# W_in's rows scaled by norm_mix, weights loaded ahead of x, a fixed TensorE order for the first row products, one PSUM layout through mix_out

## The chip, the cores and the metric

The kernel runs on one core of a Trainium2 chip. The metric is the device time of one execution in microseconds (us). An engine is named TensorE (PE), VectorE (DVE), ScalarE (ACT), GpSimd (POOL) or SyncE (SP, which issues most loads). Before the change three runs took 1360.5, 1361.68 and 1362.62 us; the median, 1361.68 us, is the time before.

## What is computed

One decoder layer on x (1024 tokens by 1024 channels, float32) with a memory of 256 tokens. Cut to what the change touches:

```python
def rms_norm(x, g):
    y = x * rsqrt(mean(x * x, axis=-1) + EPS)
    return y * g

hn = rms_norm(h, norm_mix)
proj = hn @ w_in                       # 1024 x 2320
gq, gk, gv, gr, ga, sq, sk, sv = split(proj)
o_gla = gla_mixer(gq, gk, gv, gr, ga, w_alpha, b_alpha, gla_gain)
o_swa = swa_mixer(sq, sk, sv, rel_bias, sinks)
h = h + concat([o_gla, o_swa]) @ w_out
h = h + cross_attn(rms_norm(h, norm_cross), rms_norm(mem, norm_mem), w_q_c, w_k_c, w_v_c, w_o_c)
h = h + conv_ffn(rms_norm(h, norm_ffn), w_up, conv_w, conv_b, w_down)
return rms_norm(h, norm_final)
```

`gla_mixer` is gated linear attention in chunks of 64 tokens, `swa_mixer` attention in a window of 128 tokens.

## The kernel before

**Number form.** A float32 product is made of three matmuls on a high and a low part of each operand (`mm3`: high by high, high by low, low by high). `split` makes the parts: ScalarE writes the rounded high part (L109, or L112 with a gain), DVE subtracts it from the source (L110, or L113 with a gain). A weight is loaded by SP into a stage tile `st` (L121) and split into two `w` tiles.

**Start (`rows_a`).** x arrives as eight tiles of 128 tokens (`load_x`; tiles `gr` and `prob`). TensorE transposes them into PSUM banks of the role S (`prepare_x`, L385), in groups of 1, 1, 2, 2 and 2 tiles. Each bank is copied to a tile `pts` (L388), which POOL writes to DRAM as `xt_d` (L389; it is read again for the residual), and which `split` turns, with norm_mix as gain, into the parts of x (L112, L113). `row_tile` then makes 24 matmuls per token tile, with x as the left operand and 272 columns of W_in on the right, for `ga`, `sv` and `gva`; each of these is scaled by the token's factor `rstd_x` when it leaves PSUM (L440, L442). The weights for it are nine DMAs, in three stage tiles (`row_weights`). SP issues x tile 0 first, then these nine, then x tiles 1 to 7.

**What sets the order.** In `rows_a` the tile framework's scheduler orders each engine; only the stretches under `manual_schedule` (the GLA) keep the order of the code. Each engine runs its own queue in order, so an instruction that waits holds all behind it. POOL's queue at the start holds the identity, the loads of the vectors (`vrows`, L234), the writes of `xt_d` and the masks for the attention (`masks`, L249 to L254); DVE's holds `mask_att` (L256), which reads a mask.

**After that.** `cols_swa` and `cols_gla` make the other projections transposed, a tile of 128 columns at a time, with 48 matmuls of 512 tokens; the windowed attention runs among them. The pool p2 follows, with its own PSUM layout: `gla_gates` (whose first transposes are L529), `gla_decays` (L573), `rows_b` (384 more columns of V, L136 to L138 with 384 columns), and `gla`. `gla` calls `memory`, a generator: its first part loads the two memory tiles, scales them by row (L313), transposes them (L320) and splits them into `wg`; the next parts make V (two banks of 512) and K (256 wide) of the memory for the cross attention, between the GLA's own steps, and store them through `la`. `mix_out` multiplies by W_out. `add_residual` (L866 to L874) gives the new residual, its parts `act` and its squares' sum `ss`. `rstd_of_sum` (L201, eight matmuls of one column each) and `rsqrt` (L170 and on) turn `ss` into the tokens' factors; `cross` starts with products on `act`.

**PSUM.** There are eight banks, shared by roles. Before, p1 has F=3, S=4, O=1; p2 has F=2, S=4, O=2; from mix_out on it is F=3, S=3, T=1, O=1. A pool's first use of a bank waits for the last use of the banks it lies over.

Of the kernel before, what the change touches and what calls it, by code (L numbers as in the profile page):

```python
# [16 lines left out]
F32 = mybir.dt.float32  # L18
F32R = mybir.dt.float32r
# [3 lines left out]
ALU = mybir.AluOpType  # L23
# [3 lines left out]
P = 128  # L27
# [13 lines left out]
GROUPS = (1, 1, 2, 2, 2)  # L41
# [19 lines left out]
class Layer:  # L61
# [67 lines left out]
    def load_cols(self, w, c0):  # L129

        src = w.rearrange("(kt p) c -> p kt c", p=P)[:, :, c0:c0 + P]
        return self.load([(lambda t: t, src)])
# [95 lines left out]
    def vectors(self, group, new):  # L228

        nc, base = self.nc, self.vec_at  # L230
        v = new("vrows", [P, P], bufs=2)
        at = 0
        for nm, src, n in group:
            nc.gpsimd.dma_start(out=v[at:at + n, :], in_=src.rearrange("o (n p) -> (o n) p", p=P))  # L234
            self.col[nm] = base + at
            at += n
        ps = self.bank("O")
        nc.tensor.transpose(ps[:, :at], v[:at, :], self.ident[:at, :at])
        nc.vector.tensor_copy(out=self.vec[:, base:base + at], in_=ps[:, :at])
        self.vec_at += at  # L240

    def masks(self, keep):
# [13 lines left out]
        nc.vector.tensor_scalar(out=self.mask_att, in0=self.mask_cum, scalar1=16.0, scalar2=None, op0=ALU.mult)  # L256

# [41 lines left out]
    def memory(self, new):  # L299
# [14 lines left out]
        parts = [[new("wg", [P, 3, MEM], F32R, 8) for _ in range(3)] for _ in range(2)]  # L314
        mh, ml = ([p[k // 3][:, k % 3] for k in range(NK)] for p in parts)
# [50 lines left out]
    def prepare_x(self, new):  # L366
# [4 lines left out]
        self.rstd_bc = self.bc_tile("rbx")  # L371
        self.xt_d = self.dram.tile([NK, P, T], F32, name="xt_d")
        self.x = [(self.xnew("x", dt=F32R, bufs=16), self.xnew("x", dt=F32R, bufs=16)) for _ in range(NK)]
        self.xact = self.whole(self.x)
        self.x_copies = []
        at = 0
        for n in GROUPS:
            sl = slice(at * P, (at + n) * P)
            m = 4 // n
            for k in range(0, NK, m):  # L380
                ps = self.bank("S")
                for q in range(m):
                    for i in range(n):
                        c = (q * n + i) * P
                        nc.tensor.transpose(ps[:, c:c + P], self.xr[at + i][:, (k + q) * P:(k + q + 1) * P], self.ident)  # L385
                xt = new("pts", [P, 512], bufs=9)
                copy = nc.scalar.copy if k // m % 2 else nc.vector.tensor_copy
                self.x_copies.append(copy(out=xt, in_=ps))  # L388
                nc.gpsimd.dma_start(out=self.xt_d[k:k + m, :, sl].rearrange("k p t -> p k t"),  # L389
                                    in_=xt.rearrange("p (k t) -> p k t", k=m))  # L390
                for q in range(m):
                    hi, lo = self.x[k + q]
                    h, l = self.split(xt[:, q * n * P:(q + 1) * n * P], hi[:, sl], lo[:, sl],
                                      self.v("norm_mix", k + q))
            with self.tc.issue_after(h.ins), self.tc.issue_after(l.ins):
                for i in range(at, at + n):
                    self.sumsq(self.xr[i], ssq[:, i:i + 1], T)
                self.rsqrt(self.rstd[:, at:at + n], ssq[:, at:at + n], D, n)
            yield range(at, at + n)
            at += n  # L400
            if at % 4 == 0:
                self.broadcast_rows(self.rstd, self.rstd_bc, [at // 4 - 1])


    def row_weights(self, cols, ks=range(NK), alloc=None):
# [5 lines left out]
        for g in range(ks.start, ks.stop, step):  # L411
# [5 lines left out]
            h, l = self.load(pieces, (P, m, n), alloc)  # L417
# [4 lines left out]
    def row_tile(self, i, weights, evac):  # L422

        n, hs, ls = weights
        ps = self.bank("F")
# [5 lines left out]
    def rows_a(self, keep, new):  # L431
# [13 lines left out]
        self.load_x(keep, new, range(1))  # L445
        groups = self.prepare_x(new)
        group = next(groups)
        with self.tc.issue_after(self.x_copies[0].ins), self.tc.issue_after(self.x_copies[1].ins):
            weights = self.row_weights([(1536, 16), (2192, 128), (512, 128)])
        self.load_x(keep, new, range(1, NT))  # L450
        while group:
            for i in group:
                self.row_tile(i, weights, evac)
            group = next(groups, None)

    def rows_b(self, new, first):
# [7 lines left out]
        n, hs, ls = self.row_weights([(640, 384)], range(4, NK), lambda s, sh: new("wg", sh, F32R, 8))  # L464
        for i in range(NT):
            self.row_tile(i, (n, first[1] + hs, first[2] + ls), evac)
# [29 lines left out]
    def cols_gla(self, keep):  # L496
# [3 lines left out]
        for tiles, tag, c0, n, scale in ((self.gr, "gr", 1024, 4, 1.0), (self.gk, "gk", 256, 2, 1.0),  # L500
                                         (self.gq, "gq", 0, 2, 0.125)):
            for t in range(n):
                dst = keep(tag, bufs=n)
                tiles.append(dst)
                yield from self.cols_parts(dst, self.load_cols(w, c0 + P * t), scale)

    def cols_swa(self, new):

        w = self.a["w_in"][0]
        self.sk = self.cols_in(new("sk"), self.load_cols(w, 2064), 1.0)  # L510
        self.sq = []
        wr = w.rearrange("(kt p) c -> p kt c", p=P)
        for t in range(4):
            pieces = [(lambda s, g=g: s[:, :, 64 * g:64 * g + 64],
                       wr[:, :, 1552 + 256 * g + 64 * t:1552 + 256 * g + 64 * t + 64]) for g in range(2)]
            self.sq.append(self.cols_in(new("sq", bufs=4), self.load(pieces), 0.125))
# [66 lines left out]
    def gla(self, new):  # L583
# [11 lines left out]
        memory = self.memory(new)  # L595
        next(memory)
        with self.tc.manual_schedule(engines={mybir.EngineType.PE}):
# [3 lines left out]
            for i, (early, late) in zip(range(0, NT, 2), ((2, 0), (2, 2), (2, 2), (2, 1))):  # L601
# [726 lines left out]
    def run(self):  # L1328
# [3 lines left out]
        with self.pool("xpool", "right") as self.xnew:  # L1332
            with self.pool("keep") as keep:
                with self.pool("p1") as new, self.banks(F=3, S=4, O=1):
                    self.constants()
                    self.vectors(self.vec_rows[:1], new)
                    self.rows_a(keep, new)
                    self.vectors(self.vec_rows[1:7], new)
                    self.vectors(self.vec_rows[7:], new)
                    self.masks(keep)  # L1340
                    self.swa_bias(new)
                    self.cols_swa(new)
                    self.gate_silu(self.swa(new, self.cols_gla(keep)))
# [16 lines left out]
        with psums:  # L1360
# [63 lines left out]
```

## Time and profile before

| | before |
|---|---|
| median of three runs | 1361.68 us |
| lowest, highest | 1360.5, 1362.62 us |
| the profiled execution's own time | 1360.55 us |
| its span in the profile | 1358.8 us |
| mean granted TensorE clock | 0.992 of full |
| TensorE busy | 1320.4 us (97%) |
| DVE, ScalarE, POOL busy | 899.9, 593.7, 84.7 us |
| chain that ended last | 90% TensorE, 3% DVE, 3% DMA, 2% ScalarE |

Times in the profile count from the start of the span, and the execution's own time holds 1.75 us more than the span. The chain that ended last is followed back from the last instruction, at each step to what released it. An idle time stands with the instruction that ended it, and with what that instruction had waited for. The granted clock is a share of TensorE's full speed.

### The profile page before, as it was taken

To read this page: it belongs to the slowest core of one execution; us is meant where nothing else is said; L and a number is where in the kernel's file an instruction comes from. 1 tells how busy PE (TensorE), PEld (TensorE's weight loads), DVE (VectorE), ACT (ScalarE), POOL (GpSimd) and SP (SyncE) were. 2 spreads that over 40 slices of the span, in tenths; PEclk is the share of its full clock that TensorE was granted. 3 is DMA by queue.
4 is the path that set the end of the run, shared out by engine and by line. 5 is a ranking of instruction groups with operands and counts; after the bars stand their busy time and mean duration, and the time that the engine had idled before them with its cause. 6 is when DMAs were issued, how large, how long until landed. Compare 5 with 4: busy or idle time off the path is not lost.

```text
span 1358.8 us, 17462 instructions
## 1 busy us (share of the span) xinstructions
PE 1320.4 (97%) x6635; PEld 1093.1 (80%) x6635; DVE 899.9 (66%) x1578; ACT 593.7 (44%) x1075; POOL 84.7 (6%) x142
## 2 busy tenths in 40 slices
PE   5999999999999999999999999999999999999997
PEld 5887777887888888888888888888888887888785
DVE  4626554546744444354449998888888887997776
ACT  5614546524533233354333644444444444454455
POOL 3100111000110000000110000000000000000000
PEclk8999999999999999999999999999999999999998
DMA  9442211114784511123330343222222228810203
GB/s 269 113 121 61 61 55 59 63 62 128 242 243 148 171 47 62 48 98 119 94 94 16 109 155 111 79 81 87 94 85 71 78 93 314 290 62 8 70 20 144
DMA packets 141389, 146.89 MB, mean 108 GB/s; under 512 B 15714, under 2 KB 108024, under 8 KB 141304
## 3 DMA queue, kind: packets, MB, share of 16 engines
q1 hardware_dynamic: 129974, 111.02, 26.6%
q0 software_dynamic: 10144, 32.63, 6.9%
q10 hardware_dynamic: 1186, 2.12, 0.4%
q8 instruction: 52, 0.85, 0.3%
q14 instruction: 33, 0.27, 0.1%
HBM read 109.03 MB, written 38.28 MB: 108 GB/s over the span
## 4 chain that ended last, share of the span: by engine, by line
PE 90%; DVE 3%; DMA 3%; ACT 2%; issue 1%; POOL 0%; SPq 0%; ACTq 0%; DVEq 0%; POOLq 0%
PE psS L1059 13%; PE psF L1059 13%; PE psF L136 12%; PE psF L138 12%; PE psF L137 12%; PE psF L1166 5%; PE psS L1166 5%; PE psT L1166 2%; PE psO L1166 2%; PE psO L136 1%; PE psS L136 1%; PE psS L138 1%; PE psS L137 1%; PE psO L137 1%; PE psO L138 1%; DMA act<-in_w_down_dram 1%
## 5 line engine op out<-in xcount | busy, mean ns | idle before, releaser
L109 ACT CAST w<-st 128x1024 fp32r<-128x1024 f32 (+2 forms) x165 | 145.1, 879 | 314.4 <-PE psF L137 158.5
L110 DVE TENSOR_TENSOR w<-st,w 128x1024 fp32r<-128x1024 f32 (+2 forms) x165 | 166.6, 1010 | 97.7 <-ACT w L109 95.9
L136 PE MATMUL psF<-x,w 128*128 128x512 f32 x336 | 132.6, 395 | 0.9 <-PE psS L705 0.9
L138 PE MATMUL psF<-x,w 128*128 128x512 f32 x336 | 131.3, 391 | 0.0
L137 PE MATMUL psF<-x,w 128*128 128x512 f32 x336 | 131.2, 390 | 0.0
L1088 DVE SCALAR_TENSOR_TENSOR uy<-uy,vec,uy 128x1023 f32<-128x1023 f32 (+1 forms) x88 | 112.0, 1279 | 1.3 <-ACT uy L1086 0.9
L1166 PE MATMUL psF<-w,w 128*128 128x512 f32 x330 | 92.6, 390 | 0.0
L1166 PE MATMUL psS<-w,w 128*128 128x512 f32 x330 | 92.2, 389 | 0.0
L1059 PE MATMUL psS<-a,w 128*128 128x512 f32 x360 | 86.6, 389 | 0.0
L1059 PEld LDWEIGHTS psS<-a,w 128*128 128x128 f32 x360 | 67.5, 188 | 14.3 <-ACT c L1067 0.3
L1059 PE MATMUL psF<-a,w 128*128 128x512 f32 x324 | 77.8, 389 | 0.0
L136 PEld LDWEIGHTS psF<-x,w 128*128 128x128 f32 x336 | 63.1, 188 | 16.7 <-issue 3.1
L138 PEld LDWEIGHTS psF<-x,w 128*128 128x128 f32 x336 | 63.1, 188 | 14.2 <-issue 0.6
L137 PEld LDWEIGHTS psF<-x,w 128*128 128x128 f32 x336 | 63.2, 188 | 12.6
L1166 PEld LDWEIGHTS psF<-w,w 128*128 128x128 f32 x330 | 61.8, 188 | 13.6 <-DVE w L110 0.6
L1166 PEld LDWEIGHTS psS<-w,w 128*128 128x128 f32 x330 | 61.9, 188 | 12.9
L1059 PEld LDWEIGHTS psF<-a,w 128*128 128x128 f32 x324 | 60.8, 188 | 12.6
L136 PE MATMUL psF<-act,w 128*128 128x512 f32 x176 | 69.5, 395 | 0.0
L137 PE MATMUL psF<-act,w 128*128 128x512 f32 x176 | 69.1, 392 | 0.0
L138 PE MATMUL psF<-act,w 128*128 128x512 f32 x176 | 68.7, 390 | 0.0
L1086 ACT ACTIVATE uy<-uy,vec 128x1024 f32<-128x1024 f32 x44 | 54.8, 1246 | 24.7 <-DVE uy L1079 16.9
L1059 PE MATMUL psS<-act,w 128*128 128x512 f32 x240 | 57.8, 389 | 0.0
(361 smaller groups left out, 2821.8 us busy)
## 6 DMA issues: line engine op xcount, KB each, us to landing
st<-in_w_up_dram SPq DMA_DIRECT2D x44, 512.0 KB, 4.7
g_d<-uy POOLq DMA_DIRECT2D x22, 512.0 KB, 2.9
act<-in_w_down_dram SPq DMA_DIRECT2D x12, 512.0 KB, 8.1
st<-g_d SPq DMA_DIRECT2D x10, 512.0 KB, 4.3
res<-g_d SPq DMA_DIRECT2D x10, 512.0 KB, 10.8
st<-in_w_in_dram SPq DMA_DIRECT2D x9, 512.0 KB, 4.3
xt_d<-pts POOLq DMA_DIRECT2D x16, 256.0 KB, 2.9
ow_d<-pts POOLq DMA_DIRECT2D x32, 128.0 KB, 2.7
```

The source lines that it names most:

```text
L109: h = nc.scalar.copy(out=hi, in_=src)
L110: l = nc.vector.tensor_tensor(out=lo, in0=src, in1=hi.bitcast(F32), op=ALU.subtract)
L136: mm(out, lhsT=lh, rhs=rh, start=start, stop=False)
L137: mm(out, lhsT=lh, rhs=rl, start=False, stop=False)
L138: mm(out, lhsT=ll, rhs=rh, start=False, stop=stop)
L1059: nc.tensor.matmul(ps, lhsT=b[l][:, q], rhs=a[q][r], start=first and q == 0 and n == 0, stop=first and q == 3 and n == 2, skip_group_check ...
L1086: nc.scalar.activation(out=y, in_=u, func=AF.Identity, scale=self.v("cw2", j), bias=self.v("conv_b", j))
L1088: nc.vector.scalar_tensor_tensor(out=y[:, s:], in0=u[:, :T - s], scalar=self.v(nm, j), in1=y[:, s:], op0=ALU.mult, op1=ALU.add)
L1166: nc.tensor.matmul(ps[i], lhsT=g[:, l, tk], rhs=w[:, r], start=first and k == 0 and m == 0, stop=first and k == n - 1 and m == 2, skip_gro ...
```

## The change

- norm_mix is no longer multiplied into x. Each stage tile of W_in is multiplied by the channel gains on DVE before it is split (`load` with `gains`, L124). The gain vector is loaded by ScalarE's queue instead of POOL's, and the masks are built on POOL ahead of everything else there.
- SP issues the nine weight loads before any x tile.
- A transposed bank of x is split straight from PSUM, 512 values wide (L109, L110 of the new file); no `pts` copy is made at the start. For `xt_d`, `save_x` adds high and low part (16 DVE additions, L404) and POOL writes the sums.
- TensorE's order there is written out: transposes of tiles 0 and 1, products of tile 0, transposes of tile 2, products of tile 1, and so on; the banks alternate between the roles F and O. Both halves of the factors are broadcast afterwards.
- One PSUM layout, F=2, S=4, O=2, holds from the start through mix_out. The layout F=3, S=3, T=1, O=1 opens only before `cross`.
- The memory's first part is called before `rows_b`. Its `wg` tiles are ordered by groups of channels. In the V products the two matmul triples of one bank follow each other before those of the other bank, where they alternated before. In the last round of the GLA's loop two parts of the memory, not one, run between `gla_output` and the products, so two parts are left for the end and not three.

```diff
-    def load(self, pieces, shape=(P, NK, P), alloc=None, parts=1):
+    def load(self, pieces, shape=(P, NK, P), alloc=None, parts=1, gains=None):
...
+        if gains is not None:
+            self.nc.vector.tensor_tensor(out=st, in0=st, in1=gains.unsqueeze(2).to_broadcast(list(shape)),
+                                         op=ALU.mult)
...
-        parts = [[new("wg", [P, 3, MEM], F32R, 8) for _ in range(3)] for _ in range(2)]
-        mh, ml = ([p[k // 3][:, k % 3] for k in range(NK)] for p in parts)
+        parts = [[new("wg", [P, 3, MEM], F32R, 8) for _ in range(2)] for _ in range(3)]
+        mh, ml = ([parts[k // 3][s][:, k % 3] for k in range(NK)] for s in range(2))
...
-                for q in range(2):
-                    for i in range(2):
-                        tk = slice(i * P, (i + 1) * P)
+                for i in range(2):
+                    tk = slice(i * P, (i + 1) * P)
+                    for q in range(2):
...
+        for i in range(NT):
+            tk = slice(i * P, (i + 1) * P)
+            for k in range(0, NK, 4):
+                ps = self.bank("S").rearrange("p (k t) -> p k t", k=4)
+                for q in range(4):
+                    nc.tensor.transpose(ps[:, q], self.xr[i][:, (k + q) * P:(k + q + 1) * P], self.ident)
+                h, l = self.split(ps, xh[:, k:k + 4, tk], xl[:, k:k + 4, tk])
...
+    def save_x(self, new):
...
+        for k, (hi, lo) in enumerate(self.x):
+            for h in range(2):
+                sl = slice(512 * h, 512 * h + 512)
+                t = new("pts", [P, 512], bufs=9)
+                self.nc.vector.tensor_tensor(out=t, in0=hi[:, sl].bitcast(F32), in1=lo[:, sl].bitcast(F32), op=ALU.add)
+                self.nc.gpsimd.dma_start(out=self.xt_d[k, :, sl], in_=t)
...
         self.xr = []
-        self.load_x(keep, new, range(1))
...
+        weights = self.row_weights([(1536, 16), (2192, 128), (512, 128)])
+        self.load_x(keep, new, range(NT))
+        tiles = self.prepare_x()
+        with self.tc.manual_schedule(engines={mybir.EngineType.PE}):
+            next(tiles)
+            for i in range(NT):
+                if i < NT - 1:
+                    next(tiles)
+                self.row_tile(i, weights, evac, "FO"[i % 2])
+        self.broadcast_rows(self.rstd, self.rstd_bc)
...
-            for i, (early, late) in zip(range(0, NT, 2), ((2, 0), (2, 2), (2, 2), (2, 1))):
+            for i, (early, late) in zip(range(0, NT, 2), ((2, 0), (2, 2), (2, 2), (2, 2))):
...
-                with self.pool("p1") as new, self.banks(F=3, S=4, O=1):
-                    self.constants()
-                    self.vectors(self.vec_rows[:1], new)
+                psums.enter_context(self.banks(F=2, S=4, O=2))
+                self.constants()
+                with self.pool("p1") as new:
+                    self.vectors(self.vec_rows[:1], new, self.nc.scalar)
+                    self.masks(keep)
                     self.rows_a(keep, new)
...
-                with self.pool("p2") as new, self.banks(F=2, S=4, O=2):
+                with self.pool("p2") as new:
                     self.gla_gates(new)
                     self.gla_decays(new)
-                    self.rows_b(new, first)
-                    self.gla(new)
+                    n, hs, ls = self.row_weights([(640, 384)], range(4, NK), lambda s, sh: new("wg", sh, F32R, 8))
+                    memory = self.memory(new)
+                    next(memory)
+                    self.rows_b(new, (n, first[1] + hs, first[2] + ls))
...
-            psums.enter_context(self.banks(F=3, S=3, T=1, O=1))
...
-        with psums:
+        psums.close()
+        with self.banks(F=3, S=3, T=1, O=1):
```

What moves on the engines shows in the order of their instructions, at three places. In these rows a line number is that of the file the rows are from (the new file's lines stand some four lines later), then the operation, what it writes and reads, and its size.

**DVE at the start.** Before, from the sixth split of x tile 1 (L113) on; `mask_att` waits for POOL's masks.

```order
L113 SCALAR_TENSOR_TENSOR x_106<-pts_232,vec,x_105 128x128
L113 SCALAR_TENSOR_TENSOR x_108<-pts_232,vec,x_107 128x128
L113 SCALAR_TENSOR_TENSOR x_116<-pts_138,vec,x_115 128x128
L388 COPY pts_304<-psS_299 128x512
L256 TENSOR_SCALAR mask_att_683<-mask_cum_681 128x128
L170 TENSOR_SCALAR rs_v_151<-ssq_97 128x1
L113 SCALAR_TENSOR_TENSOR x_110<-pts_248,vec,x_109 128x128
```

After, from the gain vector's copy on (`st` are the weights' stage tiles, `w` their low parts, `xl` the low part of x):

```order
L243 COPY vec<-psO_89 128x8
L260 TENSOR_SCALAR mask_att_94<-mask_cum_92 128x128
L124 TENSOR_TENSOR st_107<-st_107,vec 128x816
L124 TENSOR_TENSOR st_116<-st_116,vec 128x816
L124 TENSOR_TENSOR st_125<-st_125,vec 128x544
L110 TENSOR_TENSOR w_113<-st_107,w_112 128x816
L110 TENSOR_TENSOR xl_156<-psS_157,xh_155 128x4x128
L110 TENSOR_TENSOR w_122<-st_116,w_121 128x816
```

`mask_att` has moved ahead of the weights and of all splits of x; the gains stand ahead of the first split.

**DVE at the end of the row products.** After the change, between x tile 7's last split and the low half `w_610` of the first column tile's weight:

```order
L404 TENSOR_TENSOR pts_919<-xh_155,xl_156 128x512
L180 TENSOR_TENSOR rs_t_484<-rs_t_484,rs_v_483 128x2
L404 TENSOR_TENSOR pts_922<-xh_155,xl_156 128x512
L181 TENSOR_SCALAR rs_t_484<-rs_t_484 128x2
L404 TENSOR_TENSOR pts_925<-xh_155,xl_156 128x512
L182 TENSOR_TENSOR rstd_x<-rs_y_485,rs_t_484 128x2
L404 TENSOR_TENSOR pts_928<-xh_155,xl_156 128x512
L445 TENSOR_SCALAR sv_105<-psF_493,rstd_x 128x128
L445 TENSOR_SCALAR gva_106<-psF_493,rstd_x 128x128
L110 TENSOR_TENSOR w_610<-st_606,w_609 128x1024
```

The additions for `xt_d` are new here; six of the 16 stand before this weight, two of them ahead of these rows.

**TensorE at the cross start.** Before, from the last mix_out product on; `psO_4312` are the column sums, which run four at a time:

```order
L138 MATMUL psF_4278<-x_2656,w_4241 128x512
L201 MATMUL psO_4312<-ones,ss_3691 128x1 x4
L136 MATMUL psF_4359<-act_3692,w_4355 128x512
L137 MATMUL psF_4359<-act_3693,w_4355 128x512
L138 MATMUL psF_4359<-act_3692,w_4356 128x512
```

and 15 products further on:

```order
L138 MATMUL psF_4359<-act_4000,w_4355 128x512
L201 MATMUL psO_4312<-ones,ss_3691 128x1 x4
L136 MATMUL psF_4359<-act_4000,w_4355 128x512
L137 MATMUL psF_4359<-act_4001,w_4355 128x512
L138 MATMUL psF_4359<-act_4000,w_4356 128x512
```

After:

```order
L142 MATMUL psF_4225<-x_2673,w_4188 128x512
L205 MATMUL psO_4259<-ones,ss_3638 128x1 x8
L140 MATMUL psF_4310<-act_3639,w_4306 128x512
L141 MATMUL psF_4310<-act_3640,w_4306 128x512
L142 MATMUL psF_4310<-act_3639,w_4307 128x512
```

All eight sums now stand ahead of the first cross product.

## Rows read from the trace of the kernel before

**Rows 1.** The page, section 1: busy time, share of the span, instructions of each engine.

```profile
PE 1320.4 (97%) x6635; PEld 1093.1 (80%) x6635; DVE 899.9 (66%) x1578; ACT 593.7 (44%) x1075; POOL 84.7 (6%) x142
```

**Rows 2.** The chain of waits, 0 to 100 us: start, length, what.

```profile
2.26 4.34 DMA st<-in_w_in_dram
6.61 5.96 DMA gr<-in_x_dram
...
21.76 0.49 POOL xt_d L389
...
25.46 0.29 DVE mask_att L256
```

**Rows 3.** Timeline of TensorE, 4 to 54.6 us: start, length, instruction, [idle before <-releaser].

```profile
5.69 1.97 PE L385 MATMUL psS<-ident,gr 128*128 128x128 f32 x8
10.79 2.79 PE L385 MATMUL psS<-ident,gr 128*128 128x128 f32 x11 [3.13 <-DMA gr<-in_x_dram]
...
26.12 0.60 PE L138 MATMUL psF<-w,x 128*128 128x272 f32 x1 [6.48 <-DVE x L113]
...
45.48 1.91 PE L385 MATMUL psS<-ident,prob 128*128 128x128 f32 x16
...
52.81 0.29 PE L138 MATMUL psF<-w,x 128*128 128x272 f32 x1
...
54.07 0.40 PE L136 MATMUL psF<-x,w 128*128 128x512 f32 x1
```

**Rows 4.** Groups by shape on DVE, 5 to 54 us: busy us, mean ns | idle.

```profile
L110 DVE TENSOR_TENSOR w<-st,w 128x816 fp32r<-128x816 f32 x2 | 2.0, 1002 | 0.0
L110 DVE TENSOR_TENSOR w<-st,w 128x1024 fp32r<-128x1024 f32 x1 | 1.2, 1225 | 1.5 <-ACT w L109 1.5
L110 DVE TENSOR_TENSOR w<-st,w 128x544 fp32r<-128x544 f32 x1 | 0.7, 718 | 0.0
```

**Rows 5.** DMA issues, 0 to 30 us: count, KB each, median us to landing.

```profile
gr<-in_x_dram SPq DMA_DIRECT2D x4, 512.0 KB, 4.7
```

**Rows 6.** Table by stage: busy PE, PEld, DVE, ACT, POOL; then PEclk, DMA share, GB/s.

```profile
25.00:30.00 5.00, 3.88 (x17) 3.88 (x18) 3.81 (x18) 4.13 (x14) 2.13 (x5) 0.50 0.63 176
245.00:250.00 5.00, 4.32 (x28) 4.19 (x29) 4.68 (x7) 1.57 (x2) 2.75 (x4) 1.00 0.38 112
320.00:325.00 5.00, 4.55 (x14) 3.53 (x14) 3.03 (x7) 1.67 (x2) 1.47 (x3) 0.66 0.79 250
```

**Rows 7.** Timeline of TensorE, 240 to 380 us: the instructions behind its gaps.

```profile
245.68 1.04 PE L529 MATMUL psS<-ident,ga 128*16 128x128 f32 x8 [1.44 <-DVE pts L110]
...
295.70 1.06 PE L320 MATMUL psO<-ident,st 128*128 128x128 f32 x8 [0.75 <-DVE wg L113]
...
299.58 0.47 PE L136 MATMUL psO<-w,wg 128*128 128x512 f32 x1 [1.35 <-DVE wg L113]
...
319.16 0.47 PE L136 MATMUL psO<-w,wg 128*128 128x512 f32 x1 [1.70 <-DVE la L110]
...
320.55 0.47 PE L136 MATMUL psO<-w,wg 128*128 128x512 f32 x1 [0.45 <-DVE la L110]
...
373.67 0.39 PE L136 MATMUL psO<-wg,w 128*128 128x256 f32 x1 [0.97 <-DVE la L110]
...
378.54 0.47 PE L136 MATMUL psF<-x,w 128*128 128x512 f32 x1 [0.88 <-PE psS L705]
```

**Rows 8.** Timeline of all engines at the cross start, 464.9 to 471.3 us.

```profile
466.47 0.48 PE L136 MATMUL psF<-act,w 128*128 128x512 f32 x1
...
468.51 0.68 DVE L874 TENSOR_TENSOR ss<-ss,sq 128x512 f32<-128x512 f32 x1
...
469.96 0.95 PE L201 MATMUL psO<-ones,ss 128*128 128x1 f32 x8
470.77 0.48 PE L136 MATMUL psF<-act,w 128*128 128x512 f32 x1
470.94 0.17 DVE L170 TENSOR_SCALAR rs_v<-psO 128x8 f32<-128x8 f32 x1 [1.74 <-PE psO L201]
```

More of the change, by code (lines that the diff above doesn't have):

```diff
@@ L127, in load, with load_cols @@
         return hi, lo
[L129 removed]
+    def load_cols(self, w, c0, gains=None):
         src = w.rearrange("(kt p) c -> p kt c", p=P)[:, :, c0:c0 + P]
[L132 removed]
+        return self.load([(lambda t: t, src)], gains=gains)
     def mm3(self, out, lh, ll, rh, rl, start, stop):
@@ L226, in constants, with vectors @@
         self.vec_at = 0
-    def vectors(self, group, new):
+    def vectors(self, group, new, queue):
         nc, base = self.nc, self.vec_at
@@ L233, in vectors @@
         for nm, src, n in group:
-            nc.gpsimd.dma_start(out=v[at:at + n, :], in_=src.rearrange("o (n p) -> (o n) p", p=P))
+            queue.dma_start(out=v[at:at + n, :], in_=src.rearrange("o (n p) -> (o n) p", p=P))
             self.col[nm] = base + at
@@ L364, in load_x, with prepare_x @@
             self.xr.append(t)
-    def prepare_x(self, new):
+    def prepare_x(self):
         nc = self.nc
@@ L371, in prepare_x @@
         self.rstd_bc = self.bc_tile("rbx")
-        self.xt_d = self.dram.tile([NK, P, T], F32, name="xt_d")
[L373 to L402, printed above, removed]
@@ new lines, in prepare_x @@
+        xh, xl = (self.xnew("x" + s, (P, NK, T), F32R) for s in "hl")
+        self.x = [(xh[:, k], xl[:, k]) for k in range(NK)]
+        self.xact = self.whole(self.x)
+        for i in range(NT):
[5 more added lines that the diff above has]
+                h, l = self.split(ps, xh[:, k:k + 4, tk], xl[:, k:k + 4, tk])
+            with self.tc.issue_after(h.ins), self.tc.issue_after(l.ins):
+                self.sumsq(self.xr[i], ssq[:, i:i + 1], T)
+                if i % 2:
+                    self.rsqrt(self.rstd[:, i - 1:i + 1], ssq[:, i - 1:i + 1], D, 2)
+            yield
@@ L416, in row_weights @@
                 at += c
-            h, l = self.load(pieces, (P, m, n), alloc)
+            h, l = self.load(pieces, (P, m, n), alloc, gains=self.mix_gains(g, m))
             hs += [h[:, q] for q in range(m)]
@@ L420, in row_weights, with row_tile @@
         return n, hs, ls
-    def row_tile(self, i, weights, evac):
+    def row_tile(self, i, weights, evac, role="F"):
         n, hs, ls = weights
-        ps = self.bank("F")
+        ps = self.bank(role)
         tk = slice(i * P, (i + 1) * P)
@@ L444, in rows_a, with rows_b @@
         self.xr = []
-        self.load_x(keep, new, range(1))
[L446 to L456, printed above, removed]
+        weights = self.row_weights([(1536, 16), (2192, 128), (512, 128)])
[8 more added lines that the diff above has]
+        self.broadcast_rows(self.rstd, self.rstd_bc)
+    def rows_b(self, new, weights):
         self.gvb = [new("gvb", [P, 2, 384], bufs=4) for _ in range(NT // 2)]
@@ L462, in evac @@
                                          scalar1=self.rstd[:, i:i + 1], scalar2=None, op0=ALU.mult)
-        n, hs, ls = self.row_weights([(640, 384)], range(4, NK), lambda s, sh: new("wg", sh, F32R, 8))
         for i in range(NT):
-            self.row_tile(i, (n, first[1] + hs, first[2] + ls), evac)
+            self.row_tile(i, weights, evac)
     def gla_v(self, i, h):
@@ L515, in cols_swa @@
                        wr[:, :, 1552 + 256 * g + 64 * t:1552 + 256 * g + 64 * t + 64]) for g in range(2)]
-            self.sq.append(self.cols_in(new("sq", bufs=4), self.load(pieces), 0.125))
+            self.sq.append(self.cols_in(new("sq", bufs=4), self.load(pieces, gains=self.mix_gains(0, NK)), 0.125))
     def gla_gates(self, new):
@@ L581, in gla_decays, with gla @@
                 nc.vector.tensor_tensor(out=self.gk[t][:, sl], in0=self.gk[t][:, sl], in1=en, op=ALU.mult)
-    def gla(self, new):
+    def gla(self, new, memory):
         nc = self.nc
```

23 lines of the change are left out of this document (14 added, 9 removed).

## The prediction, written before the change was run

> **What bounds the kernel now.** I read the page first: TensorE is busy 1320.4 of 1358.8 us [rows 1]. Only its idle time, its slow stretches and its work itself can move the end, and the change leaves the matmuls of the products as they are. So I looked for TensorE's idle gaps in the timeline, for what ended them, and for the granted clock around them in the table by stage. The profiled execution took 1360.55 us, close to the lowest of the runs; the sum is made against it, and the median, 1361.68, lies 1.1 us higher.
>
> Three places count. **Start:** eight transposes of x tile 0 begin at 5.69, a wait of 3.13 us for an x tile ends at 10.79, and at 26.12 TensorE resumes after 6.48 us of nothing [rows 3]. The chain says why [rows 2]: at 21.76 POOL still issues `xt_d`, the masks come behind that in its queue, DVE waits for them with `mask_att` (25.46), and the x splits TensorE needs are queued behind that on DVE. **GLA:** seven smaller gaps from 245 to 379 us [rows 7]. **Cross start:** there TensorE does not wait [rows 8]. Cross products run from 466.47 to 469.96 while DVE still adds up the column sums' input (468.51, 0.68); the second four column sums (L201) follow at 469.96.
>
> **Clock.** The stretch from 25 to 30 us, after the 6.48 us stall, has 0.50 of the clock; the one from 320 to 325, after a stall of 1.70, has 0.66; after 1.44 the next five microseconds show 1.00 [rows 3, 6, 7]. 0.66 over 5 us is 3.4 us at the lower level (1.2 GHz of 2.4), so a stall of 1.70 us cost another 1.7.
>
> **Start, step by step.** The first columns begin at 54.07 [rows 3]. Before that lie 64 transposes (16 in 1.91 us, 0.12 each: 7.6 us) and 192 matmuls of 272 columns (ten from 52.81 to 54.07, 0.126 apart: 24.2 us), 31.8 us in all; the other 22 us are waits and slow clock. In the change SP issues nine weight loads before x tile 0, and the x load waits until the third of them has landed. A weight load that ran from 2.26 took 4.34 us [rows 2], to 6.60; with no x tile ahead of it I take 6.1. X tile 0, at the same 4.3 (the x loads' median is 4.7 [rows 5]), is there at 10.4. The transposes of tiles 0 and 1 go at the pace of the first eight, 1.97 us [rows 3] (twice that of the 16 later ones, so I read it as the lower clock): 14.4. The gains and splits of the first weights on DVE (twice 1.00, 1.00 and 0.72 [rows 4], 5.4 us) can begin when the gain vector is there, before 7 us if its load takes 4.3 too, and end by 14 with two x splits of 0.7 between them. Then the 24 products of tile 0, 3.0 us, to 17.4, and six times 0.95 and seven times 3.0: 44.2. Four broadcast matmuls, 0.5: the columns start at 44.7, 9.4 us earlier. All of this was idle or slow time, so nothing hid it.
>
> What is late next is the first column weight. On DVE six additions that rebuild x for DRAM (512 columns; 0.7 each by the 544 row [rows 4]) now stand between the last x split and that weight's low half (1.22 [rows 4]). After the last transpose: 0.7 each for the cast and the split (again the 544 row), six times 0.7, seven short operations at the 0.17 of L170 [rows 8] or little more, 1.3, then 1.2: 8.1 us. TensorE has two row tiles, the broadcasts and two products to do meanwhile, 7.0. It waits 1.1 us; bounds 0 (the additions at 0.5) and 2.5 (the second such wait, for the vectors' bank, in full). **Start: 8.3 us gained, 5 to 10.**
>
> DVE also applies the gains to 13 later W_in tiles, 1.0 to 1.2 us each [rows 4]. The products of a column tile, 48 of 0.23 us (15 in 466.47 to 469.96 [rows 8]), keep TensorE for 11 us, so I price these at nothing. Without that cover, where DVE is dense in the attention blocks, one costs its 1.2 us, twice at most.
>
> **GLA.** One PSUM layout from the start to mix_out removes the pool changes that end the gaps of 1.44 (L529 waits for DVE's `pts`) and 0.88 (L136 at 378.54). The memory rows' splits come before the row products end, so 0.75 (L320) and 1.35 (L136 at 299.58, for `wg`) go. Value products bank by bank keep the first wait for `la`, 1.70, and remove the second, 0.45. The last K product, moved, leaves 0.2 of 0.97. Together 5.6 us [rows 7]. Against it: 16 transposes among the row products wait for ScalarE's scaling of the two memory rows; priced 0.5, between 0 and 1.5 (the wait for `wg` that it replaces). The 1.70 at 319.16, and its like at 341, stay with their slow clock. **5.1 gained, 3.5 to 5.8**, and up to 3.4 more if both slow stretches vanish.
>
> **Cross start.** The cross pool now opens only after mix_out, over the banks of the old one. All eight column sums stand ahead of the first cross product, and that product's bank may be written only when DVE has read the sums (L170). In before's times: the add ends at 468.51 + 0.68 = 469.19, the sums take 0.81 (469.96 to 470.77), the read 0.17 [rows 8]: about 470.4 with hand-overs. Before, TensorE had then done the products of 466.47 to 469.96, 3.5 us, and gone on at 470.77. Loss 3.5 - (470.77 - 470.4) = 3.1; I take 3.3, as TensorE's first product waits for DVE once more. No cover is left: nothing else stands in TensorE's queue. Since 1.70 was enough for the lower clock, I add 1.7. **5.0 lost; 2.5 (DVE, alone, runs the chain 0.8 faster, and the clock holds) to 6.7 (the lower clock for twice as long).**
>
> A page of the Trainium skill speaks against the start. "DMA: Bandwidth & Descriptors" (Specifications) names 512 B as the least transfer for line rate, and the 16-column pieces of these weights have rows of 64 B; by it x would queue behind slow loads. In the trace of before the same loads stood ahead of three of the four x tiles with the median of 4.7 us [rows 5], so it bears the rule out only weakly; the case is rival A.
>
> **Sum.** 1360.55 - 8.3 - 5.1 + 5.0 = 1352.2; the forecast is **1352 us**, against a median of 1361.68. Its own range is 1347 to 1356.
>
> **Rivals.**
>
> A, *x arrives late.* If x tile 0, queued behind all nine loads, takes the 5.96 us of an x tile of before, from 6.6 [rows 2], it is there at 12.6 and not 10.4; with the first column weight at its bound the start gains 9.4 - 2.2 - 2.5 = 4.7: **1356**. For it: nine loads in the queues. Against: TensorE needs a new tile only each 4 us. 0.15.
>
> B, *stalls cost less clock.* If the cross stall leaves the clock full (1.7) and one or both slow stretches of the GLA go (1.7 each): **1347 to 1349**. For it: 1.44 cost none [rows 6, 7]. Against: the two stalls of 1.70 are as long as before. 0.15.
>
> C, *the hold-up only moves.* The change does not do what it says if POOL's queue stalls DVE again: the last seven of the 16 additions need a `pts` buffer that a DMA of POOL must have emptied, and column weights stand behind them on DVE. Price: the 6.48 us of the old stall [rows 3] and 1.7 for the clock, so 1360: **no change**. Against: POOL has its masks and vectors behind it by then, and nine buffers hold six us of additions. 0.09.
>
> D, *slower: row tiles at the lower clock.* In the fixed order TensorE waits at each tile for that tile's split, and these waits keep its clock low. A tile (8 transposes, 24 products) takes 4.0 us, at 1.2 GHz 4.0 more. It decides from the third such tile on: 2.3 use up the 9.5 us between 1352.2 and the median. Four cost 16: **1368**; all seven that remain, 1380. For it: the first eight transposes ran at half pace [rows 3]. Against: tile i+1 is transposed one row tile, 3.0 us, before its products, and its splits take DVE 1.4. 0.06.
>
> **How the numbers follow.** Forecast 0.55, A 0.15, B 0.15, C 0.09, D 0.06. About 0.2% (2.7 us) is what a measurement of this kernel can tell from no change. Faster: the forecast, A and B, 0.85; same: C, 0.09; slower: D, 0.06. The range from 1346 to 1358 takes in A, B and the bounds of the terms (all three at their worst give 1360.55 - 5 - 3.5 + 6.7 = 1358.8), and leaves out C and D.
>
> **What would show it.** Right: no gap of 6 us on TensorE before 50 us; products of 512 columns from about 45; a wait of about 1 us for the first weight's low half; no gap at L529's successor; one of about 3 us between the last mix product and the first cross product, then a clock below 1.00. Wrong: columns after 49 us, a half-speed stretch between 18 and 45, waits above 1 us for DVE in the attention blocks, or no gap at the cross start.

## The result and the profile after

| | before | after |
|---|---|---|
| median of four runs each | 1361.73 us | 1349.05 us |
| lowest, highest | 1360.5, 1362.62 | 1347.11, 1351.53 |
| ratio of the times, 95% interval | | 0.9908 (0.989 to 0.9927) |
| the profiled execution's own time | 1360.55 | 1348.35 |
| its span | 1358.8 | 1346.6 |
| TensorE busy | 1320.4 | 1315.6 |

The change is faster by 12.7 us where 9.7 was forecast (1352 against 1361.68). Where it came from is read first from fixed points of the program. The view of one source line gives the first and the last start of its instructions (last before the semicolon). These are the first scores of the windowed attention (L750 in both) and the first column sums at the cross start (L201, L205 in the new file). Kernel before:

```profile
L750 PE MATMUL psS<-sk,sq x128: 272/376/480, 111.2 to 214.3; 64*128 64x256 f32 x112, 64*128 64x128 f32 x16
L201 PE MATMUL psO<-ones,ss x32: 165/250/250, 465.7 to 708.7; 128*128 128x1 f32 x32
```

Kernel after:

```profile
L750 PE MATMUL psS<-sk,sq x128: 272/376/480, 102.5 to 205.5; 64*128 64x256 f32 x112, 64*128 64x128 f32 x16
L205 PE MATMUL psO<-ones,ss x32: 165/250/271, 448.4 to 696.2; 128*128 128x1 f32 x32
```

So the start gains 8.7 us (111.2 to 102.5), the stretch up to the cross start another 8.6 (465.7 to 448.4 is 17.3 in all), and from there to the end 5.1 are lost again, since the span is only 12.2 shorter. Forecast were 8.3, 5.1 and -5.0.

**The start.** The chain of waits of the kernel after (start, length, what) has x tile 0's load ahead of the transposes:

```profile
5.00 0.47 SPq L122
...
5.52 5.42 DMA gr<-in_x_dram
...
10.98 3.67 PE psS L389 x16
```

Its TensorE timeline, which answers [rows 3]:

```profile
10.98 3.67 PE L389 MATMUL psS<-ident,gr 128*128 128x128 f32 x16 [8.32 <-DMA gr<-in_x_dram]
14.30 0.57 PE L140 MATMUL psF<-w,xh 128*128 128x272 f32 x1
...
15.81 0.38 PE L140 MATMUL psF<-w,xh 128*128 128x272 f32 x1
16.02 0.29 PE L141 MATMUL psF<-w,xh 128*128 128x272 f32 x1
16.15 0.29 PE L142 MATMUL psF<-w,xl 128*128 128x272 f32 x1
...
45.34 0.48 PE L140 MATMUL psF<-xh,w 128*128 128x512 f32 x1
45.66 0.40 PE L141 MATMUL psF<-xl,w 128*128 128x512 f32 x1
45.89 0.44 PE L142 MATMUL psF<-xh,w 128*128 128x512 f32 x1
```

One wait of 8.32 us for x, and after it none until the columns begin at 45.34 (54.07 before). The first products come at the slow pace (about 0.22 apart) until 16.02 and at 0.126 from there.

**GLA.** The whole list of TensorE's waits from 230 to 380 us (total us, times, longest) has two lines left:

```profile
PE psO L140 <- DVE la L110: 3.8, 3, 1.7
PE psS L705 <- ACT o L693: 0.7, 3, 0.3
```

Of [rows 7] the gaps of 1.44, 0.75, 1.35, 0.45, 0.97 and 0.88 are gone; two of 1.70 stay, and one of 0.39 that stood before too (at 360.90).

**Cross start.** The timeline of all engines, which answers [rows 8]:

```profile
448.41 0.95 PE L205 MATMUL psO<-ones,ss 128*128 128x1 f32 x8
448.61 0.69 DVE L866 TENSOR_TENSOR res<-psF,res 128x512 f32<-128x512 f32 x1 [2.60 <-PE psF L142]
...
451.26 0.68 DVE L874 TENSOR_TENSOR ss<-ss,sq 128x512 f32<-128x512 f32 x1
452.00 1.07 PE L205 MATMUL psO<-ones,ss 128*128 128x1 f32 x8 [2.65 <-DVE ss L874]
453.11 0.17 DVE L174 TENSOR_SCALAR rs_v<-psO 128x8 f32<-128x8 f32 x1 [1.17 <-PE psO L205]
...
453.42 0.76 PE L140 MATMUL psF<-act,w 128*128 128x512 f32 x1 [0.35 <-DVE rs_v L174]
```

TensorE waits 2.65 us for the add and 0.35 for DVE's read, with nothing else ahead in its queue.

**Clock.** The table by stage (busy PE, PEld, DVE, ACT, POOL; then PEclk, DMA share, GB/s):

```profile
240.00:245.00 5.00, 5.00 (x24) 3.99 (x23) 1.69 (x3) 2.84 (x6) 0.11 (x1) 0.97 0.70 231
245.00:250.00 5.00, 5.00 (x22) 4.61 (x22) 1.97 (x5) 5.00 (x11) 0.00 (x0) 0.69 0.02 7
305.00:310.00 5.00, 3.11 (x16) 2.36 (x17) 3.84 (x11) 3.55 (x10) 2.06 (x3) 1.00 0.60 195
325.00:330.00 5.00, 3.30 (x27) 3.00 (x26) 4.16 (x10) 3.50 (x9) 2.07 (x3) 1.00 0.68 211
450.00:455.00 5.00, 2.65 (x12) 2.31 (x13) 3.03 (x10) 0.99 (x4) 0.24 (x1) 0.79 0.97 301
455.00:460.00 5.00, 5.00 (x21) 4.08 (x20) 0.00 (x0) 0.00 (x0) 0.00 (x0) 0.87 0.24 70
```

The two waits of 1.70 us (at 308 and 328) leave the clock full in this profile. A slow stretch stands at the GLA gates instead, where TensorE never idles, and one at the cross start. In each pair of rows the missing clock adds up to 1.7 us of TensorE's time, as 0.66 over 5 us does in [rows 6]: (0.03 + 0.31) x 5, and (0.21 + 0.13) x 5. That is called one fall from 2.4 to 1.2 GHz below.

### The profile page after: what moved, and what is told of

Read it like the earlier page. It is cut to its first block, busy times and chain, and to the rows that moved or that the text cites. A ratio compares the mean times of both kernels' runs of the same rounds, so it can differ in the third digit from the quotient of the medians.

```text
span 1346.6 us, 17402 instructions
## 1 busy us (share of the span) xinstructions
PE 1315.6 (98%) x6635; PEld 1090.7 (81%) x6635; DVE 917.1 (68%) x1577; ACT 583.7 (43%) x1041; POOL 81.0 (6%) x141
## 4 chain that ended last, share of the span: by engine, by line
PE 91%; DVE 4%; DMA 2%; ACT 2%; issue 1%; SPq 0%; ACTq 0%; DVEq 0%
PE psS L1059 13%; PE psF L1059 12%; PE psF L140 12%; PE psF L141 12%; PE psF L142 12%; PE psF L1166 5%; PE psS L1166 4%; PE psT L1166 2%; PE psO L140 2%; PE psO L1166 2%; PE psO L141 2%; PE psO L142 2%; PE psS L140 1%; PE psS L141 1%; PE psS L142 1%; DMA act<-in_w_down_dram 1%
## 5 line engine op out<-in xcount | busy, mean ns | idle before, releaser
L109 ACT CAST w<-st 128x1024 fp32r<-128x1024 f32 (+2 forms) x165 | 145.2, 880 | 335.2 <-PE psF L141 146.5
L110 DVE TENSOR_TENSOR w<-st,w 128x1024 fp32r<-128x1024 f32 (+2 forms) x165 | 166.2, 1009 | 96.6 <-ACT w L109 96.1
L140 PE MATMUL psF<-xh,w 128*128 128x512 f32 x208 | 82.7, 398 | 0.0
L141 PE MATMUL psF<-xl,w 128*128 128x512 f32 x208 | 81.4, 391 | 0.0
L142 PE MATMUL psF<-xh,w 128*128 128x512 f32 x208 | 81.3, 391 | 0.0
L1059 PEld LDWEIGHTS psF<-a,w 128*128 128x128 f32 x324 | 60.8, 188 | 12.6
L1059 PE MATMUL psS<-act,wx 128*128 128x512 f32 x240 | 57.7, 389 | 0.0
L1059 PEld LDWEIGHTS psS<-act,wx 128*128 128x128 f32 x240 | 45.1, 188 | 9.3
L1059 PEld LDWEIGHTS psS<-act,w 128*128 128x128 f32 x240 | 45.1, 188 | 9.3
```

What stands on the lines that cost most here:

```text
L109: h = nc.scalar.copy(out=hi, in_=src)
L110: l = nc.vector.tensor_tensor(out=lo, in0=src, in1=hi.bitcast(F32), op=ALU.subtract)
L140: mm(out, lhsT=lh, rhs=rh, start=start, stop=False)
L141: mm(out, lhsT=lh, rhs=rl, start=False, stop=False)
L142: mm(out, lhsT=ll, rhs=rh, start=False, stop=stop)
L1059: nc.tensor.matmul(ps, lhsT=b[l][:, q], rhs=a[q][r], start=first and q == 0 and n == 0, stop=first and q == 3 and n == 2, skip_group_check ...
```

## The experiments

Theory: three separate terms, the hold-up through the masks, the GLA's gaps, and the order of the column sums. Each run below takes one of them away or does one alone. A ratio is to the kernel before, measured on the same chip. A difference to the changed kernel is one of medians that were not measured together; where the ratios give clearly another figure, it stands beside.

**1. The sums in the cross pool.** The sums' call moves from the end of `mix_out` into the new PSUM pool, ahead of `cross`.

```diff
-        self.rc = self.rstd_of_sum(ss)
+        self.mix_ss = ss
...
                 with self.pool("cp") as cpnew:
+                    self.rc = self.rstd_of_sum(self.mix_ss)
                     self.cross(new, cpnew, o8)
```

> The changed kernel with one thing moved: the eight column sums of mix_out are issued inside the cross pool, so that TensorE's queue has four sums, twelve cross products, four sums. If the order of the sums makes the stall at the cross start (my theory: 2.65 + 0.35 us of waiting and 1.7 us of half clock), those waits fall to below 0.6 us, the clock stays at 1.00 from 445 to 460 us, and the time falls by 4.5 to 5 us, to 1344 us. If it is the layout's change itself (rival: the first bank of the new pool must wait for DVE's read), a wait for DVE of 2 us or more stays, and the gain is under 1 us. In the GLA, which is left as it is, the clock shows if its two waits of 1.70 us cost no clock here as well.

Measured: 1344.16 us, ratio 0.9874 (0.9856 to 0.9892), 4.9 below the changed kernel. In its TensorE timeline neither set of sums waits:

```profile
448.68 0.95 PE L205 MATMUL psO<-ones,ss 128*128 128x1 f32 x8
...
452.30 1.03 PE L205 MATMUL psO<-ones,ss 128*128 128x1 f32 x8
```

and the stage behind it has the full clock:

```profile
450.00:455.00 5.00, 5.00 (x27) 4.11 (x27) 3.20 (x10) 1.28 (x4) 0.52 (x1) 1.00 0.77 241
```

What the change lost at the cross start is the sums' place, and it can be had back.

**2. The banks instead.**

```diff
         with self.banks(F=3, S=3, T=1, O=1):
+            self.bank("O"), self.bank("T")
```

> The changed kernel with the cross pool's O and T banks taken first, so that the first cross product writes a bank that DVE is not reading; the order of the sums stays, eight ahead of the first product. Theory (order): only the 0.35 us wait for DVE's read goes, the 2.65 us wait stays, the time is 1348.5 to 1349. Rival (bank): 4 to 5 us less, 1344 to 1345.

Measured: 1350.56 us, ratio 0.9925 (0.9902 to 0.9947); no gain. The first cross product no longer waits, the sums before it do:

```profile
452.53 1.36 PE L205 MATMUL psO<-ones,ss 128*128 128x1 f32 x8 [2.65 <-DVE ss L874]
453.75 0.77 PE L140 MATMUL psF<-act,w 128*128 128x512 f32 x1
```

The time came out 1.5 us above the changed kernel (2.3 by the ratios, with intervals that overlap), not 0 to 0.5 below; its profile has one slow stretch more at the cross start (the table behind run 10). The wait for the bank falls as a cause.

**3. The kernel before, with the masks early.**

```diff
                     self.vectors(self.vec_rows[:1], new)
+                    self.masks(keep)
                     self.rows_a(keep, new)
                     self.vectors(self.vec_rows[1:7], new)
                     self.vectors(self.vec_rows[7:], new)
-                    self.masks(keep)
```

> The kernel before with one thing changed: the masks are built on GpSimd right after the first vector load. Theory (the hold-up through the masks is most of the start's gain): the 6.48 us gap and the half clock after it go, the first products of 512 columns begin at 46 to 48 us and not 54, the time falls by 6 to 8 us, to 1354 to 1356. Rival (the fixed order and the weights ahead of x make the gain, the hold-up only hides other waits): under 3 us, with new waits for x splits between 15 and 35 us. The GLA is that of before, so its two stretches of half clock, if bound to their waits, stand here too; if they depend on where the waits fall in time, they need not.

Measured: 1355.62 us, ratio 0.9955 (0.994 to 0.997). In its profile the first score of the attention starts 8.0 us sooner than before, of the changed kernel's 8.7:

```profile
L750 PE MATMUL psS<-sk,sq x128: 272/376/481, 103.2 to 206.3; 64*128 64x256 f32 x112, 64*128 64x128 f32 x16
```

and the stage of [rows 6] that stood at 0.50 has the full clock:

```profile
25.00:30.00 5.00, 5.00 (x43) 5.00 (x42) 4.05 (x12) 3.95 (x10) 1.51 (x2) 1.00 0.55 147
```

One line moved makes nearly all of the start's gain. The other 0.7 is less than this point differs between profiles with the start of the changed kernel (101.2 in run 1, 103.0 in run 2), so what the weights ahead of x, the gains on the weights, the fixed order and the splits straight from PSUM earn together is not shown. The time fell by less than the 8.0 us, by 5.9: the profiled execution, at 1349.69 us, is the fastest of seven, and five of the others have a lower mean clock (0.993 or 0.994, not 0.997). The two waits of 1.70 us left the clock full in this profile.

**4. x tile 0 first.** The changed kernel, with `load_x(keep, new, range(1))` ahead of `row_weights` and the other seven tiles behind it.

> The changed kernel with x tile 0 issued ahead of the nine weight loads, as before. Theory (the row products wait for x tile 1 and the weights, and tile 0 is only transposed sooner): tile 0 transposed at 5 to 7 us, first row product at 13.5 to 15 us against 14.65, time within 1.5 us of the changed kernel. Rival (weights ahead of x are worth their place): the weights come 1.3 us or more later, the row products start after 16 us, the time is 1.5 to 3 us longer.

Measured: 1348.1 us, ratio 0.9901 (0.9883 to 0.9919), 1.0 below the changed kernel, which these runs don't tell from no change. The first line is from the chain of waits, the others are from TensorE's timeline.

```profile
0.82 3.78 DMA gr<-in_x_dram
...
4.64 1.97 PE L389 MATMUL psS<-ident,gr 128*128 128x128 f32 x8 [1.48 <-DMA gr<-in_x_dram]
10.78 1.97 PE L389 MATMUL psS<-ident,gr 128*128 128x128 f32 x8 [4.17 <-DMA gr<-in_x_dram]
12.40 0.58 PE L140 MATMUL psF<-w,xh 128*128 128x272 f32 x1
```

The row products start at 12.40 and not 14.30, sooner than the theory had it (13.5 to 15). The weights were there: their place ahead of x is worth nothing that these runs show.

**5. The memory's first part late.** In the changed kernel `memory(new)` and the first `next(memory)` stand behind `rows_b` again.

> The changed kernel with the memory's first part called inside the GLA again, behind the row products, as before. Theory (the two waits for the memory's splits are hidden only by the row products): waits of about 0.75 us at the transposes of the memory rows and 1.4 us at the first V product come back, and the time rises by 2 to 2.5 us, to 1351 to 1351.5. Rival (the ordering of the wg tiles or the single PSUM layout removed them): no such waits, time within 1 us of the changed kernel. In either case this is one more look at which stretches run at half clock: at the GLA gates (seen in all four kernels with the changed GLA so far) or after the two waits of 1.70 us (seen in the kernel before alone).

Measured: 1353.18 us (1351.02 to 1353.85), ratio 0.9925 (0.9904 to 0.9945), 4.1 above the changed kernel by the medians, 2.3 by the ratios, whose intervals overlap. TensorE's timeline has both waits again:

```profile
287.39 1.06 PE L329 MATMUL psO<-ident,st 128*128 128x128 f32 x8 [0.75 <-DVE wg L113]
...
291.31 0.48 PE L140 MATMUL psO<-w,wg 128*128 128x512 f32 x1 [1.38 <-DVE wg L113]
```

The cause is as the theory had it: the waits come back, with 2.1 us. Their size in the time is not shown, as the times don't tell 2.3 from 4.1, and this profile has two falls of the clock more than the changed kernel's first one before the cross start (two at the gates and one after the first 1.70).

**6. The masks late, in the changed kernel.** `masks(keep)` stands behind the two later `vectors` calls again.

> The changed kernel with the masks called after the row products, as before. Theory (DVE was held by POOL's writes of xt_d ahead of the masks, and these are gone from there): the masks come behind the vector loads only, DVE waits less than 1 us at mask_att, and the time stays within 1 us of the changed kernel. Rival (any late mask holds DVE): a gap of 3 us or more on TensorE between 14 and 30 us, and 4 to 8 us more time.

Measured: 1349.67 us, ratio 0.991 (0.9883 to 0.9936); no difference. DVE passes `mask_att` without a wait:

```profile
17.45 0.22 DVE L260 TENSOR_SCALAR mask_att<-mask_cum 128x128 int32<-128x128 f32 x1
```

A late place of the masks alone does not hold DVE. That fits what the chain of before shows [rows 2], the early writes of `xt_d` ahead of the masks in POOL's queue. But this run has the other edits of the start too, so that moving the writes alone would do is argued and not shown.

**7. The scheduler's order.** The row products without `manual_schedule`.

> The changed kernel with the row products' TensorE order left to the scheduler. Theory (with the hold-up gone the order matters little, and the scheduler's own differs by a few rows): columns begin within 1 us of 45.3, time within 1 us of the changed kernel. Rival (the written order is what keeps TensorE busy): waits for x splits add up to 2 us or more in 15 to 45 us.

Measured: 1351.6 us, ratio 0.9914 (0.989 to 0.9939). The first product of 512 columns starts at 44.91, no wait stands between 12 and 60 us, so the written order isn't needed. The time is 2.6 above the changed kernel (0.8 by the ratios) with intervals that overlap; its profile has three falls more (below).

**8. Runs 1 and 4 together.**

> Both moves that helped or did no harm, together: the column sums issued in the cross pool (4.9 us by its own run) and x tile 0 loaded ahead of the weights (about 1 us by its own run, within the noise). Theory: they add up, 1343 us, 5.5 to 6.5 us below the changed kernel. Rival: x tile 0's place is worth nothing, 1344 us as with the sums alone.

Measured: 1342.96 us (1342.3 to 1344.53), ratio 0.9854 (0.9834 to 0.9874), 6.1 below the changed kernel (7.4 by the ratios). It is the fastest found. What it has on run 1, 1.2 us, can't be told from noise.

**9 and 10. Both kernels a second time.** No edit.

> The changed kernel, unchanged, for a second look at where its clock falls. If the falls are chance at a few places (theory: each is 3.4 us at half clock, and a place has none, one or two of them), the cross start has at least one again, and the GLA gates (240 to 250 us) and the two waits of 1.70 us may have another number than the one, none and none of the first look. If they belong to the kernel (rival), the same three places show one at the gates, none at the waits, one at the cross start.

> The kernel before, unchanged, for a second look. Theory (chance): the two waits of 1.70 us, which both had a stretch of half clock in the first look, have 0, 1 or 2 of them now; the time is 1357 to 1363 us, 1.7 us for each. Rival (bound to the second wait of 0.45 us, which only this kernel has behind the first): both stretches are there again, at 320 and 341 us.

Measured in one execution each: 1350.78 us after, 1360.27 before. The same kernels have other slow stretches. Before, second profile:

```profile
25.00:30.00 5.00, 4.11 (x18) 4.11 (x19) 4.04 (x18) 4.36 (x15) 2.02 (x5) 0.50 0.64 181
255.00:260.00 5.00, 5.00 (x21) 4.68 (x21) 2.05 (x4) 5.00 (x12) 0.00 (x0) 0.66 0.00 0
320.00:325.00 5.00, 4.35 (x13) 3.27 (x14) 4.37 (x9) 1.89 (x6) 2.42 (x4) 0.66 0.79 260
340.00:345.00 5.00, 3.30 (x29) 3.33 (x29) 4.96 (x11) 3.17 (x7) 2.74 (x4) 1.00 0.81 261
```

The stretch at 341 is gone, and one stands at the gates. After, second profile, at the cross start:

```profile
450.00:455.00 5.00, 2.78 (x12) 2.44 (x13) 2.90 (x10) 0.86 (x3) 0.11 (x1) 0.76 0.93 284
455.00:460.00 5.00, 5.00 (x15) 3.86 (x14) 0.00 (x0) 0.00 (x0) 0.00 (x0) 0.55 0.26 77
```

That is (0.24 + 0.45) x 5 = 3.45 us lost, two falls where the first profile had one, and the time is 2.4 longer. The first column sums of this profile start at 448.3:

```profile
L205 PE MATMUL psO<-ones,ss x32: 165/250/352, 448.3 to 697.7; 128*128 128x1 f32 x32
```

From there to the end of its span, 1349.0, it lost 7.6 us on the kernel before's first profile, and not 5.1. Counted this way, in falls of 1.7 us, the fourteen profiles show:

| profile | gates | first wait 1.70 | second wait 1.70 | cross start |
|---|---|---|---|---|
| before, first and second profile | 0, 1 | 1, 1 | 1, 0 | 0, 0 |
| run 3 (before, masks early) | 0 | 0 | 0 | 0 |
| after, first and second profile | 1, 1 | 0, 0 | 0, 0 | 1, 2 |
| runs 2, 4, 5 | 1, 1, 2 | 0, 0, 1 | 0, 0, 0 | 2, 2, 1 |
| runs 6, 7 | 0, 2 | 0, 0 | 0, 1 | 1, 2 |
| run 11 | 1 | 1 | 1 | 1 |
| runs 1, 8, 12 (no wait at the cross start) | 2, 1, 1 | 0, 0, 0 | 0, 1, 0 | 0, 0, 0 |

The cross start has a fall whenever it has its wait of 2.65 us (eight of eight), and none without it. At the other places the number differs between the two profiles of one kernel (before: gates 0 and 1, second wait 1 and 0), so part of it at least is chance.

**11. V products alternating.** The changed kernel with the loops over `q` and `i` of the memory's V products in the old order.

> The changed kernel with the memory's V products alternating between the two banks again, as before. Theory: the second wait for la, 0.45 us, comes back behind the first of 1.70, and costs 0.3 to 0.7 us, too little to be told from no change by the times: 1348 to 1351. Rival (the second wait decides whether the clock falls): half clock after the first wait of 1.70 us as well, 2 us or more.

Measured: 1351.58 us (1349.85 to 1354.46), ratio 0.9924 (0.9896 to 0.9952). The second wait is back:

```profile
308.14 0.47 PE L140 MATMUL psO<-w,wg 128*128 128x512 f32 x1 [1.70 <-DVE la L110]
309.54 0.47 PE L140 MATMUL psO<-w,wg 128*128 128x512 f32 x1 [0.46 <-DVE la L110]
```

This run is inconclusive. Its profile has the fall after the first wait that the rival asks for, and one after the second wait, where the edit changes nothing. Profiles with the old order of the V products (before twice, runs 3 and 11) have a fall behind the first wait in three of four cases, the others in one of ten. That speaks for a link and doesn't show one.

**12. The cross layout opened ahead of `mix_out`.**

```diff
                     self.swa_mix()
+            psums.close()
+            psums.enter_context(self.banks(F=3, S=3, T=1, O=1))
...
-        psums.close()
-        with self.banks(F=3, S=3, T=1, O=1):
+        with psums:
```

> The changed kernel with the cross layout of PSUM opened ahead of mix_out, as before. Theory: the sums stand four, fifteen products, four again, so the waits of 2.65 and 0.35 us and the half clock behind them go, and the wait of 0.88 us at the start of mix_out comes back: 4 us less than the changed kernel, 1345. Rival (one layout through mix_out gains nothing, the 0.88 us lies beside other waits): no wait at mix_out, 1344, as with the sums moved.

Measured: 1343.23 us, ratio 0.9867 (0.9846 to 0.9889), 5.8 below the changed kernel. TensorE's only wait between 345 and 375 us is this one:

```profile
345.45 0.38 PE L140 MATMUL psO<-wg,w 128*128 128x256 f32 x1 [0.39 <-DVE la L110]
```

The 0.88 us at the start of `mix_out` does not come back, so the layout alone was not its cause; the rival holds. Keeping one layout through `mix_out` thus gained nothing and cost the 5 us of the cross start.

## Why the prediction was right, point by point

- **Hold-up through the masks:** right, and nearly the whole of the start, which the working does not divide. Run 3 gives 8.0 of the 8.7 us with the masks alone. That the writes of `xt_d` ahead of them held POOL is read from the chain [rows 2]; run 6 agrees and doesn't show it alone.
- **x behind the weights:** x tile 0 took 5.42 us from its issue at 5.52, against 4.3 from 6.1 in the working: there at 10.94 and not 10.4. Nor did it wait until the third weight had landed, as the working has it: in the chain after only SP's nine issues, about 0.5 us each, stand ahead of it. The row products began at 14.30 (14.4), the columns at 45.34 (44.7). Rival A's landing of 5.96 us was nearer, but it put the arrival at 12.6, and its other half, a long wait for the first column weight, did not come. In run 4, with nothing ahead, x tile 0 took 3.78 us and was transposed from 4.64 on. The page "DMA: Bandwidth & Descriptors" of the Trainium skill (Specifications) asks for transfers of at least 512 B for the full rate, and loads with rows of 64 B stand ahead of x in the changed kernel. The traces agree in the direction: 5.42 us behind these loads, 3.78 with nothing ahead. Run 4 does not tell the width of the rows from the mere number of loads, and it moved the end by about 1.0 us.
- **First column weight:** the working's wait of 1.1 us is not there. In the DVE timeline the additions follow each other at about 0.67 us with the short operations in between, so the 1.3 us that the working adds for these were not spent, and the weight's low half came just ahead of its product at 45.89:

```profile
43.44 0.68 DVE L404 TENSOR_TENSOR pts<-xh,xl 128x512 f32<-128x512 f32 x1
44.04 0.34 DVE L445 TENSOR_SCALAR sv<-psF,rstd_x 128x128 f32<-128x128 f32 x1
44.30 0.34 DVE L445 TENSOR_SCALAR gva<-psF,rstd_x 128x128 f32<-128x128 f32 x1
44.56 2.35 DVE L110 TENSOR_TENSOR w<-st,w 128x1024 fp32r<-128x1024 f32 x2
```

- **GLA:** the gaps went as listed, and the last K product's 0.97 fully, where 0.2 was left in the working; the row products hid the memory's transposes, where 0.5 was charged. That makes 5.8 us and not 5.1. Run 5 shows the cause of 0.75 and 1.35, run 11 that of 0.45; no run takes the causes of 1.44 and 0.97 apart. One cause was wrong: the 0.88 was put down to the layout, and run 12 has the old layout there without it.
- **The step that failed** is "the 1.70 at 319.16, and its like at 341, stay with their slow clock". The waits stayed and the slow clock didn't: two falls fewer, one more at the gates, 1.7 us net. The second of the two, before:

```profile
340.00:345.00 5.00, 4.01 (x21) 4.04 (x22) 4.71 (x10) 2.17 (x6) 2.74 (x4) 0.67 0.83 271
```

That is rival B's half, and as far as the profiles show it is luck: in run 10 the stretch at 341 is gone without any edit, and ahead of the cross start the three profiles with the old GLA (before twice, run 3) have 2, 2 and 0 falls, the nine with the changed one (all but runs 5 and 11, which undo a part of it) 0 to 3, in both groups 1.3 on average. Whether the new order of the V products spares the first wait its fall stays open (run 11). 5.8 and 1.7 leave 1.1 of the 8.6 us that no listed gap accounts for; that stays open too.
- **Cross start:** 5.1 us lost where 5.0 was charged: waits of 2.65 + 0.35 for the 3.3, and one fall for the 1.7. That it came out so close is luck: four of the eight profiles with this wait have two falls there, and the second one of the changed kernel lost 7.6 us, more than the bound of 6.7. Run 1 gives it back with one call moved. Runs 2 and 12 leave the order of the sums as the cause.
- **Rivals C and D:** no sign of them. DVE never holds TensorE between 16 and 45 us, and the row tiles run at full clock from 16.02 on. The longest wait for DVE in the windowed attention is 0.4 us, so the gains on the later weights were rightly priced at nothing.

So the forecast's 1352.2 against the profile's 1348.35 is 3.5 us of the GLA, half of it the clock, and 0.4 of the start, less 0.1 at the cross start.

## What to carry to other kernels

Look for the one instruction in an in-order queue that waits for a slow neighbour's queue: here a mask that nothing reads before 301 us held the splits of x, and moving one line was worth 8.0 us at the start, of which the time kept 5.9. A pool change is cheap where other work stands in TensorE's queue, and dear where a reduction at the end of a stage is queued whole ahead of the next one; look at the order of the instructions on both sides of it. And before a slow stretch of the clock is booked to a wait, profile a second execution of the same kernel.

## What was not expected of the hardware

- The granted clock fell in a stretch in which TensorE had no idle time: the GLA gates at 245 us, 0.69 with 5.00 of 5.00 us busy, in eleven of fourteen profiles. TensorE ran 16 matmuls with 17 rows (L538, 240.93 to 244.65) just before; in all eleven profiles the fall came during them or within about 1 us of their end. No run changes them, so that they cause it is not shown.
- At the four places of the table the clock at 1.2 GHz cost nothing, 1.7 us or twice that, and the number changed between executions of one kernel. The 4.4 us between the lowest and the highest of the four runs after are of that size.
- After a wait of 1.70 us the clock fell in 8 of 28 cases, after one of 2.65 in eight of eight.
